# A z unit moved ahead of the last head's gates in a one-core encoder layer

## The chip, the core and the metric

The kernel runs on one core of a Trainium2 chip. The metric is the device time of one execution in microseconds (us). Five engines matter here: PE (TensorE, matrix products and transposes), DVE (VectorE), ACT (ScalarE), POOL (GpSimd, used here almost only to issue DMAs) and SP (SyncE, which issues most of the weight loads). Each engine works through its own instructions in the order in which the program puts them.

## The reference

One encoder layer on a sequence of 512 tokens of width 1024, all in float32:

```
mod = silu(c) @ ada_w + ada_b            # six vectors: shift1, scale1, gate1, shift2, scale2, gate2
h = rmsnorm(x, norm_mix_w) * (1 + scale1) + shift1
z, xbc, dt_raw, q, f_fwd, f_bwd, i, g = split(h @ w_in)
y_ssd = ssd_mixer(z, xbc, dt_raw, ...)   # 16 heads x 64, both directions, gated by silu(z), normed
y_hg = hgrn2_mixer(q, f_fwd, f_bwd, i, g, ...)   # 8 heads x 128, both directions, normed, gated by silu(g)
x = x + gate1 * (concat(y_ssd, y_hg) @ w_out)
h = rmsnorm(x, norm_mlp_w) * (1 + scale2) + shift2
x = x + gate2 * (relu(h @ w_up) ** 2 @ w_down)
return rmsnorm(x, final_norm_w)
```

For one HGRN2 head, forget gates `f` give decays, the keys are built from `f`, `i` gives the values V, and the state is a sum of decayed outer products of keys and values.

## The kernel before

**Units.** The input projection is cut into units of 256 weight columns, listed in `seq` and worked through by `do_unit`. A unit is named by kind and number: `i` gives the values V of two heads, `h0`, `h1`, `h2` give the gates and queries of a pair of heads, `g` and `z` the two output gates, `x` the channels of the SSD group. Heads are numbered 0 to 7; `h0 3` holds both gates of head 6, `h1 3` the queries of heads 6 and 7, `h2 3` both gates of head 7. A unit is 96 matmuls with 256 columns (`i`, `z`, `g`) or 48 with 512 (`h`, `x`). Every weight is split into two parts, `hi` (ACT) and `lo` (DVE), and each product is three matmuls. The weights of the next unit are loaded by SP into four buffers `raw` while a unit runs.

**Streams.** All other work of the mixers is written as generators: `hg_head` for a head, `ssd_group` for the SSD scan, `mix_early` and `mix_late` for the norms and transposes ahead of the output projection, `ada_sums` with `ada_gate` and `ada_T` for the vectors `gate1`, `shift2` (in the code `b2`), `scale2` (`a2`) and `gate2`. Between matmuls of a unit `tick` lets such a generator go one step on, by a hand-kept model of the engines' time (`Clock`). PE's instructions stay in exactly this order. The order on DVE, ACT and POOL is set by the tile scheduler from the same program.

**A head's end.** After seven levels on `Q2`, `K2` and `T`, a head transposes `K2` into `kt` (PE `ps_tr<-cm,K2`, ACT copies), multiplies `kt` with V (`ps_tr<-V,kt`), copies the products to S (ACT), chains them (four DVE instructions `S<-S,T`), and forms its output in `ps_sc` from `V,at` and `S,Q2`. Where a later unit needs the buffers, `ensure(hd, n)` runs a head's remaining steps at once:

```
                if what == "ff":
                    ensure(hd - 2, 99)
                    ensure(hd - 1, 2)
```

This is lines 1083 to 1085, in the h units: the gates of head 7 force the end of head 5, those of head 6 the end of head 4.

**The sums.** `ada_sums` makes 512 columns of one of the vectors on DVE: eight instructions `ada<-adaw,cact`, two for each of four loads `adaw` of 512 KB, which POOL issues into two buffers. The third load waits until the first two instructions are done, the fourth until the fourth is done. A transpose by four matmuls (`ps_tr<-ones,ada`) or one product (`ps_tr<-ada,ones`) ends a sum, and the next sum writes the same tile `ada`. The sums for gate1 (two), b2 (two) and a2 (two) may begin once head 6 is done, since they use its buffers. None begins in the last four of the sixteen steps of the output projection (line 1220). What is left of them is done at once by `bga.drain()` (line 1471), behind the first of four 256-column strips (`ps_sc`, `ps_y`, `ps_mm`, `ps_mm`; 48 matmuls each, weights `wohi`, `wolo`) that end the output projection. The vector a2 and b2 are used right after, in `h2_tile`.

Of the kernel before, what the change touches and what calls it, by code (L numbers as in the profile page):

```python
# [151 lines left out]
def encoder_layer(  # L152
# [8 lines left out]
    clock = Clock()  # L161
# [47 lines left out]
    def const(shape, name, dt=F32):  # L209
        return consts.tile(shape, dt, tag=name, name=name)  # L210
# [400 lines left out]
    def unit_load(src, cols, k0=0):  # L611

        ncols = sum(n for _, n in cols)
        quarters = []
        for q in range(4):
            raw = wp.tile([P, 544], F32, tag="raw", name=nm("raw"), bufs=4)
            v = raw[:, :2 * ncols].rearrange("p (k n) -> p k n", n=ncols)
            o = 0
            for c0_, n in cols:
                r = (k0 + 2 * q) * P  # L620
                nc.sync.dma_start(out=v[:, :, o:o + n], in_=src[r:r + 2 * P, c0_:c0_ + n].rearrange("(k p) n -> p k n", p=P))
                o += n
            quarters.append(v)
        return quarters, ncols

    def unit_split(u, qs=range(4)):
        quarters, ncols = u
        return [split(quarters[q], 2, ncols) for q in qs]
# [231 lines left out]
    def hg_head(hd, hs_):  # L860
# [78 lines left out]
                PE.transpose(out=pt[:, j * P:(j + 1) * P], in_=K2[:, half, cc * P:(cc + 1) * P], identity=ident)  # L939
            A.copy(out=kt[:, 3 * half:3 * half + 3, :], in_=pt[:, :384].rearrange("p (c n) -> p c n", n=P))  # L940
        yield
        while hd // 2 not in vready:
            yield 0.5
        vh = vpair[hd // 2][:, :, (hd % 2) * P:(hd % 2 + 1) * P]
        pts = []
# [40 lines left out]
    def hg_norm(h0, n):  # L986

        r = const([P, NT, 8], "hg_r")
        rr = r[:, :, h0:h0 + n]
        A.activation(rr, hg_ssq[:, :, h0:h0 + n], AF.Sqrt, scale=1.0 / P, bias=epsc)  # L990
        V.reciprocal(out=rr, in_=rr)
        for cc in range(NT):
            yv = hg_y[:, cc, h0 * P:(h0 + n) * P].rearrange("p (h v) -> p h v", v=P)
            V.tensor_tensor(out=yv, in0=yv, in1=rr[:, cc, :].unsqueeze(2).broadcast_to([P, n, P]), op=MULT)
# [3 lines left out]
    def mix_T(grp, j):  # L998
        src = xs if grp == 0 else hg_y
        wcol = vcol("ssdn", j) if grp == 0 else vcol("hgn", 0)  # L1000
        pt = psum("tr")
        for tt in range(NT):
            PE.transpose(out=pt[:, tt * P:(tt + 1) * P], in_=src[:, tt, j * P:(j + 1) * P], identity=ident)
        hi, lo = m_hi[grp][:, j, :], m_lo[grp][:, j, :]
        A.activation(hi, pt, AF.Copy, scale=wcol)
        V.scalar_tensor_tensor(out=lo, in0=pt, scalar=wcol, in1=hi.bitcast(F32), op0=MULT, op1=SUB)

    def mix_early():

        hg_norm(0, 6)  # L1010
        yield
        for j in range(6):
            mix_T(1, j)
            yield
# [4 lines left out]
    vpair, vready, heads = {}, set(), {}  # L1019
# [10 lines left out]
    def do_unit(kind, arg, w, last):  # L1030
# [46 lines left out]
        else:  # L1077
            for j, (what, hd) in enumerate(hparts(kind, arg)):
                hs_ = heads.setdefault(hd, {})
                if j:  # L1080
                    pend.append(last)
                o = mm_T(w, j, h_hi, h_lo, hook=tick)
# [3 lines that stand above are left out]
                hg_evac(hd, what, o, hs_)  # L1086
                hs_["n"] = hs_.get("n", 0) + 1
                if hs_["n"] == 3:
                    ensure(hd - 2, 99)
                    steps[hd] = 0  # L1090
                    hs_["gen"] = counted(hd, hg_head(hd, hs_))
                    sth[hd % 2].add(hs_["gen"], hs_["q"], hs_["K2"], hs_["T"])
                tick()

    steps = {}
# [10 lines left out]
    def ensure(hd, n):  # L1106

        if hd < 0:
            return
        st_ = sth[hd % 2]  # L1110
        while steps.get(hd, 1000) < n and st_.advance():
            pass
# [7 lines left out]
    def hparts(kind, pr):  # L1120
# [4 lines left out]
    seq = [("i", 0), ("h0", 0), ("h1", 0), ("x", 1), ("g", 0), ("h2", 0), ("x", 2),  # L1125
# [4 lines left out]

    def ucols(u):
        k, a = u
        if k in ("h0", "h1", "h2"):
            return [(cols[w_] + hd * P, P) for w_, hd in hparts(k, a)]
        cl = [(cols[k] + a * 256, 256)]
        if u == ("i", 0):
            cl.append((O_DT, 16))
        return cl

    w = unit_split(unit_load(w_in2, ucols(seq[0])))  # L1140
    for i, u in enumerate(seq):
        nw = []
        if i + 1 < len(seq):
            nxt = unit_load(w_in2, ucols(seq[i + 1]))
            nw = unit_split(nxt, range(3))
        if u == ("i", 1):
            ensure(1, 99)
        if u == ("i", 2):
            ensure(3, 99)
        if u == ("i", 3):  # L1150
            ensure(5, 99)
        if u[0] == "z" and not z_phase[0] and (u[1] == 2 or not sts.gens):
            z_phase[0] = True
            sts.drain()
            ssds.close()
            ypl = yps.enter_context(tc.tile_pool(name="ypl", bufs=1, side="right", reuse_waits="tile"))
            m_hi[1] = ypl.tile([P, KD, T], F32R, tag="B_hi", name="m_hi1")
            m_lo[1] = ypl.tile([P, KD, T], F32R, tag="B_lo", name="m_lo1")
            ensure(5, 99)
            stc.add(mix_early())  # L1160

        def last():
            if nw:
                nw.extend(unit_split(nxt, range(3, 4)))
        do_unit(u[0], u[1], w, last)
        w = nw
# [446 lines left out]
    for fb_ in range(NF):  # L1613
        for s_ in range(NS):
            g = fb_ * NS + s_
# [79 lines left out]
```

## Time and profile before

| | |
|---|---|
| median of 3 runs | 976.21 us (974.95 to 1007.0) |
| the profiled execution's own time | 975.98 us |
| its span, first to last instruction | 974.2 us (1.8 us lie outside the span) |
| mean granted TensorE clock | 0.991 |
| PE busy | 937.1 us (96%) |
| weight loads of PE (PEld) | 816.6 us (84%) |
| DVE busy | 729.4 us (75%) |
| ACT busy | 535.5 us (55%) |
| POOL busy | 48.0 us (5%) |

PE is busy nearly all the time, so the places where it is not are few and can be read one by one. In the rows of the trace in order of time, the columns are the start and the duration in us, engine, line of the kernel, operation, output<-input, and the count of instructions merged into the row; in brackets stand the idle time of the engine just before and what released it. All instructions of PE have line 170 or 175 and those of DVE and ACT line 106, since helpers issue them, so the tiles' names tell the place. In a name the buffer's number is left out (K and Q are `K2` and `Q2`).

### The profile page before, as it was taken

The numbers are of one execution on the slowest core, as the hardware profiler recorded it, in microseconds if no ns is written. First come the engines' busy times: TensorE is split into PE (matmuls) and PEld (weight loads), VectorE is DVE, ScalarE is ACT, GpSimd is POOL, SyncE is SP. The second block draws the span as 40 slices with busy tenths as digits, with TensorE's granted clock in tenths as the row PEclk, the third lists the DMA queues.
The fourth block names the chain that finished last, engine by engine and source line by source line (L and its number), as shares of the span: only waits on it lengthen the run. The fifth ranks groups of instructions, "written<-read, shape, count | busy, mean of one in ns | idle before, by whom it ended". The sixth has DMA issues, their size and how long they took to land.

```text
span 974.2 us, 17637 instructions
## 1 busy us (share of the span) xinstructions
PE 937.1 (96%) x6846; PEld 816.6 (84%) x6846; DVE 729.4 (75%) x1269; ACT 535.5 (55%) x1007; POOL 48.0 (5%) x91
## 2 busy tenths in 40 slices
PE   5999999999999999989999999889999999999997
PEld 4788887788877887879997899878799889889987
DVE  4588869787989586867866676897788568667845
ACT  6367647756676466565655324746237326523824
POOL 0000000011000000000111210000000000000000
PEclk8999999999999999999999999999999999999999
DMA  8963422334422343222556786425324313512222
GB/s 270 261 156 84 115 77 59 94 88 125 123 68 67 106 127 94 66 76 67 182 166 187 265 277 190 140 89 161 97 87 141 108 34 108 162 56 87 87 66 87
DMA packets 111865, 119.33 MB, mean 122 GB/s; under 512 B 8188, under 2 KB 93349, under 8 KB 111781
## 3 DMA queue, kind: packets, MB, share of 16 engines
q1 hardware_dynamic: 103285, 89.07, 31.5%
q0 software_dynamic: 8064, 28.32, 9.4%
q8 instruction: 54, 0.88, 0.4%
q10 hardware_dynamic: 432, 0.82, 0.2%
q14 instruction: 30, 0.25, 0.1%
HBM read 116.01 MB, written 2.16 MB: 121 GB/s over the span
## 4 chain that ended last, share of the span: by engine, by line
PE 83%; DVE 6%; ACT 4%; DMA 4%; issue 2%; SPq 1%; DVEq 0%; ACTq 0%; POOLq 0%
PE ps_mm L170 44%; PE ps_sc L170 24%; PE ps_y L170 9%; PE ps_tr L170 4%; PE ps_tr L175 1%; DMA e<-cdr 1%; DVE t L106 1%; DVE lo L106 1%; ACT hi L106 1%; DMA raw<-in_w_out_dram 1%; DMA xe<-in_w_up_dram 1%; DVE x L106 1%; ACT xn L106 1%; DVE ada L106 1%; SPq L230 1%
## 5 line engine op out<-in xcount | busy, mean ns | idle before, releaser
L106 ACT CAST hi<-raw 128x512 fp32r<-128x512 f32 (+1 forms) x220 | 132.3, 612 | 159.4 <-PE ps_sc L170 74.9
L106 DVE TENSOR_TENSOR lo<-raw,hi 128x512 fp32r<-128x512 f32 (+1 forms) x220 | 146.2, 679 | 85.0 <-ACT hi L106 83.5
L170 PE MATMUL ps_mm<-hi,h_hi 128*128 128x256 f32 (+1 forms) x384 | 114.3, 298 | 0.0
L106 ACT CAST hi<-xr 128x512 fp32r<-128x512 f32 x100 | 59.1, 619 | 90.1 <-PE ps_y L170 41.3
L170 PE MATMUL ps_mm<-lo,h_hi 128*128 128x256 f32 (+1 forms) x384 | 108.2, 282 | 0.0
L170 PE MATMUL ps_mm<-hi,h_lo 128*128 128x256 f32 (+1 forms) x384 | 108.1, 282 | 0.0
L170 PE MATMUL ps_mm<-h_hi,hi 128*128 128x512 f32 x256 | 107.4, 420 | 0.0
L170 PE MATMUL ps_mm<-h_lo,hi 128*128 128x512 f32 x256 | 101.2, 395 | 0.2 <-DVE h_lo L106 0.2
L170 PE MATMUL ps_mm<-h_hi,lo 128*128 128x512 f32 x256 | 101.2, 395 | 0.0
L106 DVE TENSOR_TENSOR lo<-xr,hi 128x512 fp32r<-128x512 f32 x100 | 66.5, 686 | 21.6 <-ACT hi L106 21.0
L170 PEld LDWEIGHTS ps_mm<-hi,h_hi 128*128 128x128 f32 x384 | 72.4, 189 | 3.5 <-issue 1.7
L170 PEld LDWEIGHTS ps_mm<-lo,h_hi 128*128 128x128 f32 x384 | 72.5, 189 | 1.9 <-issue 1.7
L170 PEld LDWEIGHTS ps_mm<-hi,h_lo 128*128 128x128 f32 x384 | 72.4, 189 | 0.0
L170 PEld LDWEIGHTS ps_mm<-h_hi,hi 128*128 128x128 f32 x256 | 48.2, 188 | 15.6 <-issue 2.3
L170 PEld LDWEIGHTS ps_mm<-h_lo,hi 128*128 128x128 f32 x256 | 48.2, 188 | 11.7 <-issue 1.4
L170 PEld LDWEIGHTS ps_mm<-h_hi,lo 128*128 128x128 f32 x256 | 48.1, 188 | 10.9
L106 DVE SCALAR_TENSOR_TENSOR ada<-adaw,cact,ada 128x512 f32<-128x512 f32 x56 | 42.0, 749 | 16.1 <-DMA adaw<-in_ada_w_dram 15.4
L170 PE MATMUL ps_mm<-hi,uh 128*128 128x512 f32 (+1 forms) x144 | 50.3, 349 | 0.9 <-DVE t L106 0.9
L106 DVE TENSOR_TENSOR Q<-Q,T 128x512 f32<-128x512 f32 x56 | 42.0, 750 | 11.6 <-PE ps_sc L170 11.5
L170 PE MATMUL ps_mm<-hi,ul 128*128 128x512 f32 (+1 forms) x144 | 49.4, 343 | 0.0
L170 PE MATMUL ps_mm<-lo,uh 128*128 128x512 f32 (+1 forms) x144 | 49.2, 342 | 0.0
L106 ACT ACT_TABLE_LOAD x37 | 47.5, 1283 | 1.4 <-PEq L1682 0.7
(362 smaller groups left out, 2507.5 us busy)
## 6 DMA issues: line engine op xcount, KB each, us to landing
raw<-in_w_in_dram SPq DMA_DIRECT2D x68, 256.0 KB, 3.1
adaw<-in_ada_w_dram POOLq DMA_DIRECT2D x32, 512.0 KB, 5.1
raw<-in_w_down_dram SPq DMA_DIRECT2D x64, 256.0 KB, 2.9
xr<-in_w_up_dram SPq DMA_DIRECT2D x30, 512.0 KB, 3.8
raw<-in_w_in_dram SPq DMA_DIRECT2D x104, 128.0 KB, 2.7
ada_in<-in_ada_w_dram SPq DMA_DIRECT2D x16, 512.0 KB, 6.0
e<-cdr POOLq DMA_DIRECT2D x32, 256.0 KB, 3.7
raw<-in_w_out_dram SPq DMA_DIRECT2D x32, 256.0 KB, 5.0
```

The lines of the kernel that those rows point to most:

```text
L106: return f(*args, **kw)
L170: return tc.keep_in_program_order(nc.tensor.matmul(**kw))
L175: return tc.keep_in_program_order(nc.tensor.transpose(**kw))
L230: nc.sync.dma_start(out=raw[:, :n], in_=w_in2[kc * P:(kc + 1) * P, c0_:c0_ + n])
```

## The change

Four edits. The unit `z 0` stands ahead of `h2 3` in `seq`, where it stood behind `i 3`. A head's products with V are put off while the modelled time of V's copy plus 1.0 lies ahead of PE's modelled time. At the start of the z phase `ensure(5, 99)` is gone, and `mix_early` waits in its place until heads 4 and 5 are through.

```diff
@@ hg_head
-        while hd // 2 not in vready:
+        while hd // 2 not in vready or clock.at(vpair[hd // 2]) + 1.0 > clock.pe:
             yield 0.5
         vh = vpair[hd // 2][:, :, (hd % 2) * P:(hd % 2 + 1) * P]
@@ mix_early
+        while min(steps[4], steps[5]) < 1000:
+            yield 0.5
         hg_norm(0, 6)
@@ seq
-           ("h0", 3), ("h1", 3), ("g", 3), ("h2", 3), ("i", 3),
-           ("z", 0), ("z", 1), ("z", 2), ("z", 3)]
+           ("h0", 3), ("h1", 3), ("g", 3), ("z", 0), ("h2", 3), ("i", 3),
+           ("z", 1), ("z", 2), ("z", 3)]
@@ start of the z phase
-            ensure(5, 99)
             stc.add(mix_early())
```

No instruction is added or removed; what changes is the order. A program with the third and fourth of the named edits alone (no `ensure(5, 99)`, the wait in `mix_early`) has the rows of before on PE and DVE, and a program without these two has the rows of the change: in both orders heads 4 and 5 are through before the z phase begins. On SP the four loads of z 0 now stand ahead of the eight of h2 3 and the four of i 3.

The first place is PE at the end of head 5. Before, in `h2 3`, its last steps stand in one piece behind the first gate's product (`ps_mm`):

```order
L170 MATMUL ps_sc_4627<-Q_674_3852,K_647_3697 64x64 x8
L175 MATMUL ps_tr_4644<-cm,K_647_3697 128x128 x3
L175 MATMUL ps_tr_4649<-cm,K_647_3697 128x128 x3
L170 MATMUL ps_tr_4654<-V_3802,kt_4643 128x128 x3
L170 MATMUL ps_tr_4658<-V_3802,kt_4643 128x128 x3
L170 MATMUL ps_sc_4669<-V_3802,at_3919 128x128
L170 MATMUL ps_sc_4669<-S_4662,Q_674_3852 128x128
```

In the change they are spread over the second half of `z 0`, with twelve or more matmuls between two of them. These are the rows from the products with V:

```order
L170 MATMUL ps_tr_4724<-V_3802,kt_4697 128x128 x3
L170 MATMUL ps_tr_4728<-V_3802,kt_4697 128x128 x3
L170 MATMUL ps_sc_4739<-Q_757_4309,hy_4679 64x64 x8
L170 MATMUL ps_mm_4632<-hi_4292,h_hi 128x256
L170 MATMUL ps_mm_4632<-lo_4293,h_hi 128x256
L170 MATMUL ps_mm_4632<-hi_4292,h_lo 128x256
L170 MATMUL ps_mm_4632<-hi_4292,h_hi 128x256
```

Twelve 256-column and six 512-column matmuls stand there ahead of the outputs from `S,Q2`. For head 4 the products with V moved likewise: before they stood right behind the last matmul of `i 2`, whose result is V; now they stand inside `h0 3`, behind eighteen of the 48 matmuls, and six more 512-column matmuls stand between them and the head's outputs, which line 1084 forces there.

The second place is DVE at the end of head 7, in the z units. Before, the four instructions `S<-S,T` stand ahead of the sum for the second half of gate1 (`ada_5512`):

```order
L106 SCALAR_TENSOR_TENSOR S_5488<-S_5488,T_5361 128x128 x4
L106 TENSOR_TENSOR hold_5205<-hold_5205,ps_tr_5495 128x512
L106 TENSOR_SCALAR ada_5512<-adaw_5513,cact 128x512
L106 SCALAR_TENSOR_TENSOR ada_5512<-adaw_5513,cact,ada_5512 128x512
L106 SCALAR_TENSOR_TENSOR ada_5512<-adaw_5515,cact,ada_5512 128x512 x2
```

In the change they stand among the instructions of that sum (`ada_5609`) on its third and fourth loads:

```order
L106 TENSOR_SCALAR ada_5609<-adaw_5610,cact 128x512
L106 SCALAR_TENSOR_TENSOR ada_5609<-adaw_5610,cact,ada_5609 128x512
L106 SCALAR_TENSOR_TENSOR ada_5609<-adaw_5612,cact,ada_5609 128x512 x2
L106 TENSOR_TENSOR xs<-xs,t_5626 128x2x256
L106 SCALAR_TENSOR_TENSOR ada_5609<-adaw_5690,cact,ada_5609 128x512
L106 SCALAR_TENSOR_TENSOR S_5639<-S_5639,T_5554 128x128
L106 SCALAR_TENSOR_TENSOR ada_5609<-adaw_5690,cact,ada_5609 128x512
L106 SCALAR_TENSOR_TENSOR S_5639<-S_5639,T_5554 128x128 x2
L106 SCALAR_TENSOR_TENSOR ada_5609<-adaw_5694,cact,ada_5609 128x512
```

The first S row now stands behind the first instruction on the third load, the last S row behind the first instruction on the fourth.

The third place is the end of the output projection, behind the first strip (`ps_sc_6575` before, `ps_sc_6552` in the change). Before, PE has one set of four matmuls there, the last a2 sum's:

```order
L170 MATMUL ps_sc_6575<-wohi_6485,m_hi_5000 128x256
L170 MATMUL ps_sc_6575<-wolo_6486,m_hi_5000 128x256
L170 MATMUL ps_sc_6575<-wohi_6485,m_lo_5001 128x256
L170 MATMUL ps_tr_6632<-ones,ada_6218 128x1 x4
L170 MATMUL ps_y_6660<-wohi_6251,m_hi_5000 128x256
```

In the change both a2 sums end there, since head 6 ends one unit later and with it the start of all the sums:

```order
L170 MATMUL ps_sc_6552<-wohi_6462,m_hi_5132 128x256
L170 MATMUL ps_sc_6552<-wolo_6463,m_hi_5132 128x256
L170 MATMUL ps_sc_6552<-wohi_6462,m_lo_5133 128x256
L170 MATMUL ps_tr_6609<-ones,ada_6195 128x1 x4
L170 MATMUL ps_tr_6632<-ones,ada_6615 128x1 x4
L170 MATMUL ps_y_6660<-wohi_6228,m_hi_5132 128x256
```

On DVE all eight instructions of the second of them (`ada_6615`) stand behind the reading of the first one's result (`a<-ps_tr`):

```order
L106 TENSOR_TENSOR t_6601<-ps_sc_6552,hold_5607 128x256
L106 TENSOR_TENSOR a_671<-ps_tr_6609,vt 128x4
L106 TENSOR_TENSOR x_6115<-x_6115,t_6601 128x256
L106 TENSOR_SCALAR ada_6615<-adaw_6616,cact 128x512
L106 SCALAR_TENSOR_TENSOR ada_6615<-adaw_6616,cact,ada_6615 128x512
L106 RECIPROCAL rs_6504<-rs_6504 128x1
L106 SCALAR_TENSOR_TENSOR ada_6615<-adaw_6618,cact,ada_6615 128x512
L106 TENSOR_SCALAR xn_6502<-x_6115,rs_6504 128x512
L106 SCALAR_TENSOR_TENSOR ada_6615<-adaw_6618,cact,ada_6615 128x512
L106 SCALAR_TENSOR_TENSOR ada_6615<-adaw_6622,cact,ada_6615 128x512 x2
L106 SCALAR_TENSOR_TENSOR ada_6615<-adaw_6626,cact,ada_6615 128x512 x2
L106 TENSOR_TENSOR a_671<-ps_tr_6632,vt 128x4
```

Before, the corresponding sum (`ada_6218`) is spread over the stretch of the output projection ahead of the strips (its columns 512 to 767), and this place holds the sum for the first half of gate2 (`ada_7597`), whose product stands much later on PE.

## The prediction

> **What bounds the kernel now.** I read the page first, then the list of PE's waits, then the timeline of PE where it waits.
>
> ```profile
> PE 937.1 (96%) x6846; PEld 816.6 (84%) x6846; DVE 729.4 (75%) x1269; ACT 535.5 (55%) x1007; POOL 48.0 (5%) x91
> PE 83%; DVE 6%; ACT 4%; DMA 4%; issue 2%; SPq 1%; DVEq 0%; ACTq 0%; POOLq 0%
> ```
>
> The first row is busy time, the second the chain that ended last. PE carries the time; an edit that moves its work gains only what PE loses in waiting, and costs whatever new waiting it makes. So I price waits, each at its place. In the stretch that the change reorders (heads 4 to 7 and the output projection, 357 to 620 us) PE waits here:
>
> ```profile
> 359.21 1.78 PE L170 MATMUL ps_tr<-V,kt 128*128 128x128 f32 x8 [1.92 <-ACT V L106]
> ...
> 419.81 0.87 PE L175 MATMUL ps_tr<-cm,K 128*128 128x128 f32 x6 [0.80 <-DVE K L106]
> 420.92 1.60 PE L170 MATMUL ps_tr<-V,kt 128*128 128x128 f32 x12 [0.24 <-ACT kt L106]
> ...
> 425.10 0.46 PE L170 MATMUL ps_sc<-S,Q 128*128 128x128 f32 x2 [2.35 <-DVE S L106]
> ...
> 488.63 1.13 PE L170 MATMUL ps_tr<-ada,ones 128*128 128x512 f32 x2 [0.62 <-ACT S L106]
> ```
>
> The first is head 4, whose products follow the last matmul of V; the next three are head 5, ended in one piece; the last is a sum's product queued behind head 7's copies. Together 5.9 us, 0.6% of the time: that is all that the change can win directly.
>
> **Head 5: -3.4 us.** The three waits (0.80 + 0.24 + 2.35) come from work done at once. In the order of the change twelve 256-column matmuls stand between the transposes and the products with V, and a level product, twelve such matmuls and six 512-column ones behind them.
>
> ```profile
> 394.47 0.28 PE L170 MATMUL ps_mm<-lo,h_hi 128*128 128x256 f32 x1
> 394.59 0.27 PE L170 MATMUL ps_mm<-hi,h_lo 128*128 128x256 f32 x1
> ...
> 388.21 0.39 PE L170 MATMUL ps_mm<-h_lo,hi 128*128 128x512 f32 x1
> 388.44 0.39 PE L170 MATMUL ps_mm<-h_hi,lo 128*128 128x512 f32 x1
> ```
>
> Start to start these are 0.12 and 0.23 us, so the cover is 1.4 us for kt and over 2.8 us for S, against waits of 0.24 and 2.35. I take the whole 3.4; the bounds are 1.0 (a queue on DVE in z 0 eats most of the cover of S) and 3.4. The z unit's own work is the same wherever it stands. Its four loads go ahead of eight others on SP's queue and need the same buffers; PE waits for no weight part in this stretch, so I cost them at nothing; without that cover a late load of such a unit would cost about the page's median landing.
>
> **Head 4: -1.6 us.** The wait for V goes, but what is late next? In the new order PE meets the SSD products, eighteen matmuls, the products with V, six matmuls, then S.
>
> ```profile
> 385.12 1.10 PE L170 MATMUL ps_y<-xs,e 128*64 128x64 f32 x32
> 386.15 1.98 PE L170 MATMUL ps_sc<-st,ct 128*128 128x512 f32 x4
> 387.57 0.79 PE L170 MATMUL ps_mm<-h_hi,hi 128*128 128x512 f32 x1
> ...
> 392.25 0.69 PE L170 MATMUL ps_sc<-Q,hy 128*64 128x64 f32 x16
> ...
> 359.71 0.69 DVE L106 TENSOR_TENSOR lo<-raw,hi 128x512 fp32r<-128x512 f32 x1
> ...
> 366.39 0.69 DVE L106 TENSOR_TENSOR e<-e,off 128x512 f32<-128x512 f32 x1
> 367.00 0.68 DVE L106 TENSOR_TENSOR xs<-xs,t 128x512 f32<-128x512 f32 x1
> ...
> 423.56 1.39 DVE L106 SCALAR_TENSOR_TENSOR S<-S,T 128x128 f32<-128x128 f32 x4 [3.00 <-ACT S L106]
> ...
> 369.72 0.38 PE L170 MATMUL ps_sc<-V,at 128*128 128x128 f32 x2
> ```
>
> PE is free at 359.21 - 1.92 = 357.3; SSD products 387.57 - 385.12 = 2.45; eighteen matmuls 4.1; a level product 0.6; products with V 422.36 - 420.92 = 1.4 by the rows of head 5; six matmuls 1.4; the first output product 0.2: it asks for S at about 367.5. On DVE the new order puts thirteen instructions between the last `lo` (done 360.4) and S, at about 0.61 start to start: S begins at 368.3 and ends at 369.7. So 2.2 us of waiting for S take the place of the 1.92 for V. Before, PE began these outputs at 369.72 with six 512-column matmuls of the unit still behind them (1.4 us); now it begins them at 369.7, with none behind. With the 0.2 us of the first V product already done, that is 1.6 us earlier. Bounds: 0, if the wait for S is 1.6 us longer, and 3.7, if S is in time.
>
> **Head 7: +1.9, and the product behind it -0.6 us.** The 0.62 at 488.63 goes, since that product no longer stands behind head 7's. But S now waits in DVE's queue behind the sum.
>
> ```profile
> 490.52 0.48 DVE L106 TENSOR_SCALAR ada<-adaw,cact 128x512 f32<-128x512 f32 x1
> ...
> 498.95 0.75 DVE L106 SCALAR_TENSOR_TENSOR ada<-adaw,cact,ada 128x512 f32<-128x512 f32 x1 [0.71 <-DMA adaw<-in_ada_w_dram]
> DMA to landing us min/median/max: 3.9/5.1/7.4
> ```
>
> From the product's start to the sum's first instruction 490.52 - 488.63 = 1.9 us; the fourth load's first instruction comes 8.4 us after that; the last S behind it ends another 1.0 us later: 11.3. PE has the product (1.1), 24 matmuls (2.9), transposes (0.9), products with V (1.4), 24 matmuls (2.9), 0.2: 9.4. It waits 1.9 us. Bounds 0 (loads at the fast end) and 4.2 (the last at 7.4 instead of 5.1).
>
> **The end of the output projection: +15.3 us.** This is the largest term. PE's queue now holds two sums' matmuls between the first and the second strip. The second sum writes the tile that the first one's matmuls read, so all eight of its instructions come after them, and PE, whose order is fixed, stands until they are done. The trace shows what such a sum takes at this very place, since gate2's stands there before:
>
> ```profile
> 593.38 0.95 PE L170 MATMUL ps_tr<-ones,ada 128*128 128x1 f32 x8
> ...
> 598.78 0.41 DVE L106 TENSOR_TENSOR t<-ps_sc,hold 128x256 f32<-128x256 f32 x1
> 599.11 0.14 DVE L106 TENSOR_TENSOR a<-ps_tr,vt 128x4 f32<-128x4 f32 x1
> ...
> 599.63 0.48 DVE L106 TENSOR_SCALAR ada<-adaw,cact 128x512 f32<-128x512 f32 x1
> ...
> 605.40 0.75 DVE L106 SCALAR_TENSOR_TENSOR ada<-adaw,cact,ada 128x512 f32<-128x512 f32 x1 [2.61 <-DMA adaw<-in_ada_w_dram]
> ...
> 608.16 0.76 DVE L106 SCALAR_TENSOR_TENSOR ada<-adaw,cact,ada 128x512 f32<-128x512 f32 x1 [0.68 <-DMA adaw<-in_ada_w_dram]
> 601.20 0.71 POOL L436 DMA_DIRECT2D adaw<-in_ada_w_dram  x1 [17.66 <-DVE rs L106]
> 603.08 0.72 POOL L436 DMA_DIRECT2D adaw<-in_ada_w_dram  x1 [1.18 <-DVE ada L106]
> ```
>
> DVE reaches the place 5 us after PE (599.1 against 594.3), as it still has evacuations and weight parts to do; the work on DVE ahead of it is the same in the change (one sum there either way), so I keep 599.6. Two loads are there; the third is issued at 601.2, when its buffer comes free, and used at 605.4; the fourth lets its first instruction begin at 608.16, and two instructions at 0.67 and 0.75 end the sum at 609.6. PE stands from 594.3 to 609.6: 15.3 us. The second set of matmuls itself adds nothing, since the first has only moved here. Bounds: 10.2, if DVE has caught up and begins the sum at 594.5, and 17.6, with a landing of 7.4.
>
> [...]
>
> **The clock behind the gap: +1.6 us.** The granted clock halves behind some of the waits:
>
> ```profile
> 360.00:361.00 1.00, 1.00 (x7) 0.78 (x8) 0.77 (x3) 0.27 (x1) 0.00 (x0) 0.50 0.77 194
> ...
> 363.00:364.00 1.00, 1.00 (x3) 0.52 (x4) 1.00 (x3) 0.00 (x0) 0.54 (x1) 1.00 0.43 144
> ...
> 638.97 0.39 PE L170 MATMUL ps_y<-m_hi,lo 128*128 128x256 f32 x1 [2.32 <-DVE lo L106]
> ...
> 640.00:641.00 1.00, 1.00 (x7) 1.00 (x6) 1.00 (x3) 0.00 (x0) 0.00 (x0) 0.50 0.08 16
> ```
>
> In these stretches of 1 us the seventh figure is the clock: 0.50 after the waits of 1.92 and 2.32, full again some 3.2 us later, so about 1.6 us of work lost. A gap of 15 us will surely do it. Bounds 0 and 1.7. [...]
>
> **What the gap gives back: -3.6 us.** Behind the strips PE waits for the norm of the new x:
>
> ```profile
> 601.79 1.12 PE L175 MATMUL ps_tr<-cm,xn 128*128 128x128 f32 x8 [0.66 <-ACT xn L106]
> 610.43 1.09 PE L175 MATMUL ps_tr<-cm,xn 128*128 128x128 f32 x8 [1.85 <-ACT xn L106]
> 616.88 0.39 PE L170 MATMUL ps_mm<-m_hi,hi 128*128 128x256 f32 x1 [0.71 <-ACT m_hi L106]
> 617.61 0.38 PE L170 MATMUL ps_mm<-m_lo,hi 128*128 128x256 f32 x1 [0.34 <-DVE m_lo L106]
> ```
>
> All four (3.56) come from DVE's lag of 5 us, which the gap clears. Bounds: 0, and 8.0 if the wait of 2.32 at 638.97 and two smaller ones near it go too; they come from DVE's own work there, so I leave them in.
>
> **Sum.** -3.4 - 1.6 + 1.9 - 0.6 + 15.3 + 1.6 - 3.6 = +9.6 us on the profiled execution's 975.98, which lies 0.23 us from the median: 985.6 us, 1.0% slower.
>
> **Rivals.**
>
> - *The gap is not on the path.* If PE finds the second sum ready, as it finds a2's last sum at 593.38 before, the last three terms fall away, and 975.98 - 3.7 = 972.3 us remain, faster by 0.4%. For it speaks that the second sum's first two loads can be there early; against it that the tile is single, so the sum cannot start before PE's first set. 0.10.
> - *The heads' waits come back elsewhere.* If S of head 5 is as late as S of head 4 and each new wait of 2 us halves the clock for 3.2 us (1.6 each, heads 4 and 7), the gain of 3.4 shrinks to 1.0 and 3.2 are added: 985.6 + 2.4 + 3.2 = 991.2. For it speaks the clock behind 359.21; against it that the wait of 2.35 at 425.10 is followed by a full clock. 0.16.
> - *Slower by over 2%.* The sum's loads: if DVE reaches the place later by as much as PE is early, and both awaited loads land at 7.4, the gap is 17.6, and with nothing given back the total is 985.6 + 2.3 + 3.6 = 991.5; only with the second rival on top, 997, does it pass 995.5. 0.04.
> - *The change does less than it says:* two of the four edits move nothing, as the order shows. This costs nothing and is part of every case.
>
> **Chances and range.** The forecast, 0.70: with a gap of 10.2 it gives 980.5, with one of 17.6 it gives 987.9, and the heads' bounds add some 2 us on either side, so 978 to 990; the first three rivals 0.10, 0.16 and 0.04. The range takes 977 to 993, that is the forecast and most of the second rival; the first, at 972, stays out. Since 2% is about what a measurement of this kernel can tell from no change: faster 0.01, same 0.95, slower 0.04.
>
> **What would show it.** Right: a wait of about 15 us on PE for DVE `ada` between the first and second strip, a clock of 0.50 for some 3 us behind it, no wait over 0.5 us for xn behind that; no three waits in a row for K, kt and S of head 5; waits of about 2 us for S at heads 4 and 7. Wrong: matmuls of the strips running on without a gap, which would make the time about 972; a gap of 10 us, if DVE had no lag, which would make it about 980.

## The result and the profile after

| | before | the change |
|---|---|---|
| median | 975.58 us (6 runs) | 993.17 us (6 runs, 992.15 to 994.8) |
| ratio | | 1.0172, 95% interval 1.0154 to 1.0191 |
| the profiled execution's own time, span | 975.98, 974.2 us | 992.15, 990.4 us |
| mean granted TensorE clock | 0.991 | 0.981 |

The change makes the kernel 1.7% slower. The forecast was 1.0% slower, 985.6 us, and the measured median lies just above the upper end of its range, 993. The slowdown is below the 2% within which the forecast put 0.95 of its chances; the interval is 0.4% wide, so a measurement of this kernel tells far smaller differences apart than the 2% that the forecast named for it. (The two medians give 1.0180, inside the interval.) Runs over 1.5% above the fastest of the same kernel, here one of before with 1007.0 us, are left out of the ratios here and below.

The page's rows of busy time and of the chain that ended last, of the change:

```profile
PE 940.4 (95%) x6846; PEld 820.4 (83%) x6846; DVE 730.8 (74%) x1269; ACT 534.6 (54%) x1007; POOL 48.0 (5%) x91
PE 78%; DVE 8%; DMA 6%; ACT 4%; issue 3%; SPq 0%; DVEq 0%; ACTq 0%; POOLq 0%
```

PE has the same 6846 matmuls and is busy for 3.3 us more, though no matmul was added: the granted clock was lower, 0.981 against 0.991. In the chain PE's share fell from 83 to 78%, and DVE and DMA took it over. The waits of PE, from its timeline in the change:

```profile
369.48 0.46 PE L170 MATMUL ps_sc<-S,Q 128*128 128x128 f32 x2 [1.39 <-DVE S L106]
503.46 0.46 PE L170 MATMUL ps_sc<-S,Q 128*128 128x128 f32 x2 [2.34 <-DVE S L106]
511.49 0.50 PE L170 MATMUL ps_mm<-hi,m_hi 128*128 128x512 f32 x1 [2.24 <-ACT t L106]
532.96 1.31 PE L175 MATMUL ps_tr<-cm,xs 128*128 128x128 f32 x8 [1.05 <-DVE m_lo L106]
541.95 1.05 PE L170 MATMUL ps_tr<-ones,ada 128*128 128x1 f32 x8 [0.57 <-DVE m_lo L106]
594.51 0.95 PE L170 MATMUL ps_tr<-ones,ada 128*128 128x1 f32 x8
610.63 1.86 PE L170 MATMUL ps_tr<-ones,ada 128*128 128x1 f32 x8 [15.17 <-DVE ada L106]
```

The three waits of head 5, the wait for V of head 4, the one for a product behind head 7's copies and all four behind the strips are gone. New are the two waits for S (heads 4 and 7), the gap of 15.17 us between the last two sets of `ones,ada`, all three foreseen, and the waits for ACT's `t` at 511.49 and for `m_lo` at 532.96, which the forecast did not have. (`t` is what ACT writes when it empties a bank of products, `xn` the normed new x, `m_hi` and `m_lo` are the two parts of a stage's input, `lo` is the second part of a weight, and `r` a product of the first MLP stage ahead of its relu.)

To see where the time went, the program is cut at three matmuls that stand at the same place of the work in every kernel. The first row below is the first matmul of the output projection before; then come, for the change, that matmul and the first one of the stage behind the strips (before, it is the row at 616.88 in the prediction). The third cut is the set of `ones,ada` behind the first strip, at 594.51 above and at 593.38 in the prediction.

```profile
512.58 0.40 PE L170 MATMUL ps_mm<-hi,m_hi 128*128 128x512 f32 x1
```
```profile
508.39 0.40 PE L170 MATMUL ps_mm<-hi,m_hi 128*128 128x512 f32 x1
634.06 0.28 PE L170 MATMUL ps_mm<-m_hi,hi 128*128 128x256 f32 x1
```

| stretch (us) | before | the change | difference | forecast |
|---|---|---|---|---|
| start to output projection | 512.58 | 508.39 | -4.2 | -3.7 |
| from there to the set of `ones,ada` behind the first strip | 80.80 | 86.12 | +5.3 | 0 |
| from there to the stage behind the strips | 23.50 | 39.55 | +16.05 | 15.3 + 1.6 - 3.6 = +13.3 |
| from there to the last instruction | 357.3 | 356.3 | -1.0 | 0 |
| sum | | | +16.2 | +9.6 |

The sum is that of the two profiled executions; the medians differ by 17.6. The forecast failed in the second row, and by less in the third.

### The profile page after: what moved, and what is told of

Same layout as the page of the kernel before. It is cut to its first block, busy times and chain, and to the rows that moved or that the text cites. A ratio compares the mean times of both kernels' runs of the same rounds, so it can differ in the third digit from the quotient of the medians.

```text
span 990.4 us, 17626 instructions
## 1 busy us (share of the span) xinstructions
PE 940.4 (95%) x6846; PEld 820.4 (83%) x6846; DVE 730.8 (74%) x1269; ACT 534.6 (54%) x1007; POOL 48.0 (5%) x91
## 4 chain that ended last, share of the span: by engine, by line
PE 78%; DVE 8%; DMA 6%; ACT 4%; issue 3%; SPq 0%; DVEq 0%; ACTq 0%; POOLq 0%
PE ps_mm L170 41%; PE ps_sc L170 23%; PE ps_y L170 9%; PE ps_tr L170 4%; DMA adaw<-in_ada_w_dram 3%; DMA raw<-in_w_in_dram 1%; DVE ada L106 1%; DVE lo L106 1%; PE ps_tr L175 1%; ACT hi L106 1%; DVE t L106 1%; DMA e<-cdr 1%; DMA raw<-in_w_out_dram 1%; DMA raw<-in_w_up_dram 1%; ACT xn L106 1%
```

## The experiments

Each kernel's ratio is to before, measured on the same chip. Kernels with the same instructions up to the output projection reached it anywhere from 508.4 to 514.4 us in their traces, and a trace is one execution, so effects of a few us are read from the stretches of the table above, and the ratios only where the effect is larger than some 3 us.

### Each half alone

Only the edit on V's copy (the line in `hg_head`), and only the edit on `seq`:

```diff
-        while hd // 2 not in vready:
+        while hd // 2 not in vready or clock.at(vpair[hd // 2]) + 1.0 > clock.pe:
```

> Before, with only the edit that holds a head's products with V until the modelled time of V's copy. Theory: no gap behind the first strip (one set of ones,ada there); at head 4 a wait for S of 1.4 us, as in the trace of the change, stands in place of the 1.92 for V and the half clock of 3.4 us behind it; head 5 keeps its three waits. 975.6 - 1.92 + 1.39 - 1.5 (the half clock) - 0.6 (products no longer waiting) = 973.0 us, plus or minus 1.2. Rival (the prediction's first working, without the clock): 974.0. Rival (the later end of head 4 pushes a later wait by as much): 975.6.

Measured: ratio 0.9972, interval 0.9958 to 0.9987. PE's waits at heads 4 and 5:

```profile
370.04 0.46 PE L170 MATMUL ps_sc<-S,Q 128*128 128x128 f32 x2 [1.70 <-DVE S L106]
416.38 1.60 PE L170 MATMUL ps_tr<-V,kt 128*128 128x128 f32 x12 [0.24 <-ACT kt L106]
420.55 0.46 PE L170 MATMUL ps_sc<-S,Q 128*128 128x128 f32 x2 [2.35 <-DVE S L106]
```

The wait for V is replaced by one of 1.70 for S, without a stretch of half clock behind it (the mean granted clock is 0.995 against 0.991); there is no gap. Of head 5's three waits the one for K is gone too, and an earlier one for xn behind the strips (0.66 before), while a wait of 0.62 for ACT's S appears at 462.15. 0.9972 of 975.6 is 972.9, the theory's 973.0, but the interval (971.5 to 974.3) also holds the first rival, 974.0 without the clock. This edit alone is a small gain, and the fastest kernel of this study.

```diff
-           ("h0", 3), ("h1", 3), ("g", 3), ("h2", 3), ("i", 3),
-           ("z", 0), ("z", 1), ("z", 2), ("z", 3)]
+           ("h0", 3), ("h1", 3), ("g", 3), ("z", 0), ("h2", 3), ("i", 3),
+           ("z", 1), ("z", 2), ("z", 3)]
```

> Before, with only the unit z 0 moved in front of the eighth head's gates. Theory (the move alone delays the end of head 6 and with it all sums): two sets of ones,ada behind the first strip with a wait for ada of about 15 us, three waits of head 5 gone, wait for V of head 4 kept or turned into one at the copy's end: 994 us, plus or minus 2. Rival (the gap takes both edits): no wait for ada, 975.6 - 3.4 = 972.2 us.

Measured: 1.0117, interval 1.0082 to 1.0153, that is 987 where before is 975.6; 994 was expected. The waits of PE:

```profile
359.45 0.82 PE L170 MATMUL ps_tr<-V,kt 128*128 128x128 f32 x5 [2.16 <-ACT V L106]
510.74 0.50 PE L170 MATMUL ps_mm<-hi,m_hi 128*128 128x512 f32 x1 [1.38 <-ACT t L106]
608.38 1.87 PE L170 MATMUL ps_tr<-ones,ada 128*128 128x1 f32 x8 [15.78 <-DVE ada L106]
```

The move of z 0 alone makes the gap. Against the whole change it lacks head 7's wait for S (2.34), 0.86 of the wait for `t`, and the stretch of half clock behind that wait (512.75 to 516.16 in the change): its output projection up to the gap takes 83.14 us against 86.12. On DVE, this kernel has head 7's four S together, ahead of the sum's instruction on its third load at 501.50:

```profile
498.53 1.22 DVE L106 SCALAR_TENSOR_TENSOR S<-S,T 128x128 f32<-128x128 f32 x4
```

The order on PE differs as well: here the sum's product stands behind head 7's transposes (494.00 and 492.40), in the change ahead of them (492.22 and 494.50). So the edit on V, a gain by itself, seems to cost something once z 0 is moved: head 7's products stand behind the sum's, its S falls in among the sums' instructions, and what follows head 7 comes late (its norm on ACT at 509.23, here at 506.92). The ratios bear this out only just: the interval of the change, 1.0154 to 1.0191, begins where this one ends.

### The gap behind the first strip

The limit for starting a new sum set later, so that one set only stands behind the strip:

```diff
-            ada_on[0] = i < 12 or not ada_idle[0]
+            ada_on[0] = i < 14 or not ada_idle[0]
```

> The change, with the limit for starting a new sum in the output projection set two steps later (14 instead of 12 of sixteen), so that the first a2 sum ends inside the output projection, as before the change, and one sum is left behind the first strip. Theory (the gap is a queue of two sums in one tile): PE's wait of 15.2 us for ada goes, and with it the half clock from 598.1 to 618.6 in the trace of the change, which cost PE about 3.3 us of work; the waits for xn and m_hi behind the strips come back (3.6 us in the trace of before). 993.2 - 15.2 - 3.3 + 3.6 = 978.3 us, plus or minus 1.5. Rival (DVE is late there whatever stands in its queue, and the gap only collects it): a wait for ada of 5 to 10 us stays, and the time is 983 to 988.

Measured: 1.0079, interval 1.0051 to 1.0107, or 983.3 where before is 975.6. The theory, 978.3, missed. The rival's range holds the time, and a wait of 5 us stays, but not where the rival had it. PE's rows at the last two sets:

```profile
573.86 1.84 PE L170 MATMUL ps_tr<-ones,ada 128*128 128x1 f32 x8 [5.41 <-DVE ada L106]
605.20 0.95 PE L170 MATMUL ps_tr<-ones,ada 128*128 128x1 f32 x8
```

The last sum is ready when PE asks for it. The wait is at the sum before it, which is now ended at once after the sixteenth step, 5.41 us too early for it; the clock is halved for 6.8 us there. Of the waits behind the strips 2.0 us come back (0.95 for xn, 0.70 for m_hi, 0.34 for m_lo). Sums that start late are waited for wherever the program ends them.

All sums allowed only after head 7, which puts three sets behind the strip:

```diff
-        if hd == 6:
+        if hd == 7:
```

> The change, with all the sums allowed only after head 7 instead of head 6: three sets of ones,ada then stand behind the first strip on PE, and no sum stands among head 7's S on DVE. Theory (each sum queued there costs PE its whole length): the gap grows by one sum, 10.0 us of DVE by the trace of the change and 1.9 for a set on PE, to about 27; in return the wait for S of 2.3 at head 7, the 2.24 for t at the start of the output projection and the half clock behind that (1.6) go: 993.2 + 11.9 - 6.1 = 999, ratio 1.023, plus or minus 0.003. Rival (the gap is one fixed lag of DVE that any number of sums fits into): the gap stays near 15, ratio 1.011.

Measured: 1.0205, interval 1.0188 to 1.0221, or 995.6 where before is 975.6. PE's rows at head 7's outputs, at the start of the output projection and at the second and third set behind the strip:

```profile
498.68 0.39 PE L170 MATMUL ps_sc<-S,Q 128*128 128x128 f32 x2
508.46 0.50 PE L170 MATMUL ps_mm<-hi,m_hi 128*128 128x512 f32 x1 [1.22 <-ACT t L106]
604.01 1.87 PE L170 MATMUL ps_tr<-ones,ada 128*128 128x1 f32 x8 [14.73 <-DVE ada L106]
616.47 1.84 PE L170 MATMUL ps_tr<-ones,ada 128*128 128x1 f32 x8 [10.59 <-DVE ada L106]
```

One more sum in the queue is one more wait of 10.6 us, the length of a sum, so the first 14.7 fits a sum of 10 and a lag of 5, as the forecast had it. The first row has no wait in brackets: with no sum among them on DVE, head 7's S are in time. Of the wait for `t` half stays.

The last set of `ones,ada` on PE put behind the second strip, the sum itself issued where it was (`ada_n` counts the multiplications of the sums that are issued, 48 in all):

```diff
         if tt == 0:
-            bga.drain()
+            while ada_n[0] < 48:
+                bga.advance()
+        if tt == 1:
+            bga.drain()
```

> The change, with the last set of ones,ada on PE put behind the second strip instead of the first; the sum on DVE is issued at the same place as in the change. Theory (the gap is the time from PE's arrival to the sum's end, and anything put into it is free): one strip of 48 matmuls at 0.118 us, 5.7 us, runs inside the gap; the wait for ada falls from 15.2 to about 9.5, the half clock behind it stays; 993.2 - 5.7 = 987.5, ratio 1.0113. Rival (the second strip's evacuation and norm stand behind the sum on DVE, so that PE waits for xn later by what it gained): ratio 1.015 to 1.017.

Measured: 1.0105, interval 1.0079 to 1.0132, the theory's 1.0113. PE's row:

```profile
617.10 1.86 PE L170 MATMUL ps_tr<-ones,ada 128*128 128x1 f32 x8 [10.11 <-DVE ada L106]
```

The strip runs inside the gap; 10.11 are left of 15.17, and no wait for xn comes back. So the gap lies on the path, and what is put into it is free.

### What sets the sum's start

The last sum in a tile of its own:

```diff
-    ada_tile[1] = lambda: mp.tile([P, T], F32, tag="ada", name=nm("ada"))
+    n_acc = [0]
+    def acc_tile():
+        n_acc[0] += 1
+        return xn2[:, 3, T:] if n_acc[0] == 2 else mp.tile([P, T], F32, tag="ada", name=nm("ada"))
+    ada_tile[1] = acc_tile
```

> The change, with the last a2 sum in a tile of its own (the free half of the last row of xn), so that it need not wait for PE's first set of ones,ada. Theory (DVE's queue, 5 us behind PE, sets when the sum starts; the single tile does not): the sum starts some 1.3 us earlier than in the trace of the change, only because it now stands ahead of the strip's evacuation on DVE; the wait of 15.2 becomes 13.5 to 14.5, ratio 1.016. Rival (the single tile holds the sum): the sum starts with its first loads in place, before 595 us, the wait falls to 9 or 10, ratio 1.011 to 1.012.

Measured: 1.0181, interval 1.0165 to 1.0196. PE's row, DVE's where the sum begins (its tile is called xn here), and ACT's just before:

```profile
612.16 1.83 PE L170 MATMUL ps_tr<-ones,xn 128*128 128x1 f32 x8 [16.07 <-DVE xn L106]
```
```profile
602.04 0.15 DVE L106 TENSOR_SCALAR ssq<-ssq 128x1 f32<-128x1 f32 x1 [0.40 <-ACT xn L106]
602.11 0.48 DVE L106 TENSOR_SCALAR xn<-adaw,cact 128x512 f32<-128x512 f32 x1
```
```profile
601.07 0.84 ACT L106 ACTIVATE xn<-x 128x768 f32<-128x768 f32 x1 [0.21 <-DVE x L106]
```

With this tile the sum still starts 7.0 us after PE's first set (595.14); in the change it starts 6.1 us after it (600.59 against 594.51). That the gap would shorten to 13.5 to 14.5 was wrong. But the kernel does not settle what holds the sum. Its tile is columns 512 to 1023 of the last row of xn, and the squares that ACT forms for the norm write columns 0 to 767 of that row (`row_head`). The ACT row above is the fourth such write, hence of that row; it ends at 601.91, and the sum begins at 602.11. So the sum was cut loose from one tile and tied to another. What the trace of the change itself shows is that its tile is free when PE's first set ends, at 595.46, and that DVE takes up the sum 5.1 us later, with 0.9 us of idle time in between: for so long it is DVE's queue that holds it. Whether a tile that nobody else uses would let it start earlier stays open.

### The clock behind the gap

PE kept busy in the gap by 58 matmuls that the result does not need:

```diff
             acc = yield from ada_sums(which, q)
+            if which == 4 and q == 1:
+                pw = psum("tr")
+                for _ in range(58):
+                    PE.matmul(out=pw, lhsT=m_hi[1][:, 1, :P], rhs=m_hi[1][:, 0, :], start=True, stop=True)
```

> The change, with 58 matmuls of 512 columns between the two last sets of ones,ada on PE, into a bank that nobody reads; this adds work that the result does not need, so that PE is busy for about 13.4 us of the 15.2 us gap. Theory (the clock halves because PE is idle, and stays halved for 8 us behind the gap): the sum on DVE ends at the same time, the granted clock stays at 1.00 through the strips, and 3.3 us come back: 993.2 - 3.3 = 989.9 us, plus or minus 0.7. Rival (the half clock behind the gap costs nothing, since PE would then wait for the norm of the new x, as it did for 3.2 us before the change): waits of 2 to 3 us for xn or m_hi appear behind the strips, and the time stays within 0.7 us of 993.2.

Measured: 1.0168, interval 1.014 to 1.0196, the same as the change. In the two-microsecond windows below (the seventh figure is the clock, in brackets the count of matmuls), first the strips of the change, then those of this kernel:

```profile
612.00:614.00 2.00, 2.00 (x11) 2.00 (x10) 1.36 (x5) 0.00 (x0) 0.00 (x0) 0.50 0.76 223
616.00:618.00 2.00, 2.00 (x11) 2.00 (x11) 0.56 (x1) 0.00 (x0) 0.71 (x1) 0.50 0.91 252
620.00:622.00 2.00, 2.00 (x19) 2.00 (x19) 1.15 (x4) 0.00 (x0) 0.72 (x1) 1.00 0.21 72
```
```profile
616.00:618.00 2.00, 2.00 (x19) 2.00 (x18) 1.35 (x4) 0.00 (x0) 0.29 (x1) 1.00 0.81 250
671.60 0.55 PE L170 MATMUL ps_sc<-m_hi,hi 128*128 128x256 f32 x1 [2.02 <-DVE r L106]
```

At half clock PE starts 11 strip matmuls in 2 us, at full clock 19, a loss of 42%; from its return at 610.63 to 618.56 that is 3.3 us. The filled gap has no half clock (1.00 from 616 to 618 us; the 2.71 us for which PE still waits there fall into two slices of 3.41 us, cut as in the last section, and the first, from 610.11, is idle for 55%), and from the second set to the next stage it takes 19.8 us against 23.4. But the total is not less: between the two sets it takes 0.8 more, and behind the strips 2.4 more, of which 1.5 is in waits for DVE: 0.95 more for r (2.02 against 1.07), 0.3 more for lo and 0.31 for m_lo. The theory was right on the clock and wrong on the time; the rival was right on the time, though its waits for xn and m_hi did not come. What keeps the rest of the gain from showing stays open; a stretch of half clock of 3.4 us stands behind the strips in both kernels (from 656.11 in the change, from 671.55 here).

### The start of the output projection

What ACT does when PE waits for `t`, in the change (ACT's timeline):

```profile
506.76 1.15 ACT L106 CAST hi<-raw 128x512 fp32r<-128x512 f32 x2
507.93 1.28 ACT L106 ACT_TABLE_LOAD   x1
509.23 0.30 ACT L106 ACTIVATE hg_r<-hg_ssq,epsc 128x8 f32<-128x8 f32 x1
509.55 1.28 ACT L106 ACT_TABLE_LOAD   x1
510.84 0.60 ACT L106 ACTIVATE t<-ps_mm 128x512 f32<-128x512 f32 x1
```

The last z products leave their bank with the silu at 510.84. Ahead of it stand the norm of heads 6 and 7 and a table load on each side of it. In before the norm stands at 497.32, in a lull; since head 7 ends late, it now falls on the end of the z phase. This kernel ties the norm to the last z unit:

```diff
-        A.activation(rr, hg_ssq[:, :, h0:h0 + n], AF.Sqrt, scale=1.0 / P, bias=epsc)
+        eb = epsc
+        if h0:
+            eb = const([P, 1], "eps_late")
+            V.tensor_scalar(out=eb, in0=zssq[:, 3, 3:4], scalar1=0.0, scalar2=EPS, op0=MULT, op1=ADD)
+        A.activation(rr, hg_ssq[:, :, h0:h0 + n], AF.Sqrt, scale=1.0 / P, bias=eb)
```

> The change, with the norm of heads 6 and 7 tied to the last z unit (its eps is made by one small DVE instruction from a sum that the last z evacuation writes), so that ACT evacuates the last z products first and computes the norm afterwards. The change itself stood at 1.0172 of before. Theory (PE's wait of 2.24 us for ACT's t at the start of the output projection comes from ACT's two table loads and the norm ahead of the evacuation, and half the clock for 3.4 us with it): both go, 2.24 + 1.6 = 3.8 us, ratio 1.013, plus or minus 0.0015. Rival (the start of the output projection is early anyway, and the time comes back at the next wait for m_lo or in the gap behind the first strip, whose end DVE sets): ratio 1.016 to 1.018.

Measured: 1.0168, interval 1.0142 to 1.0194. By the ratio nothing is gained: the theory's 1.013 lies outside the interval, and the rival's range, 1.016 to 1.018, holds the time. The trace shows the wait gone all the same: ACT evacuates first,

```profile
514.43 0.60 ACT L106 ACTIVATE t<-ps_mm 128x512 f32<-128x512 f32 x1
516.72 1.28 ACT L106 ACT_TABLE_LOAD   x1
518.01 0.30 ACT L106 ACTIVATE hg_r<-hg_ssq,eps_late 128x8 f32<-128x8 f32 x1
```

PE has no wait for `t`, and from the first matmul of the output projection to the set behind the first strip it takes 82.54 us (514.23 to 596.77) against 86.12. That is 3.6 of the 3.8 expected. In this trace 0.6 of it went into a longer gap (15.81), and PE reached the output projection 5.8 us later than in the change, with two stretches of half clock on the way, behind the waits for S of heads 4 and 7, that the trace of the change does not have (its mean granted clock is 0.979 against 0.981). So the cost of the norm's place is shown in its own stretch, and not in the time of this kernel, whose five runs spread from 988.7 to 996.4 us.

Then both, the norm tied to the last z unit and the last set behind the second strip, and a third kernel in which the set stands further back, behind 39 of the third strip's 48 matmuls (the expectation says 36; the trace counts 39); the change itself ran beside them. The third kernel's edit, besides the norm's and, behind the first strip, the `while` loop shown above in place of the drain:

```diff
-            if i == 2 and tt >= 2:
-                h2_tile(tt - 2)
+            if i == 12 and tt == 2:
+                bga.drain()
+            if i == 14 and tt == 2:
+                h2_tile(0)
+            if i == 2 and tt == 3:
+                h2_tile(1)
```

> The change itself once more, beside the next two on one chip. Ratio 1.017, plus or minus 0.002; in the trace a gap of 15 to 16 us behind the first strip, a wait of about 2.2 us for ACT's t at the start of the output projection; stretches of half clock that last whole multiples of 3.41 us and start only behind a stretch of 3.41 us in which PE was idle for more than about half.

> The change, with the last set of ones,ada behind the second strip and the norm of heads 6 and 7 behind the last z evacuation. Theory (the two costs lie at different places and add): the first alone stood at 1.0105; the wait for t (2.2) and the half clock behind it (1.5) go as well: ratio 1.0067, plus or minus 0.002. Rival (DVE, not PE, sets the time from the start of the output projection to the sum's end, so an earlier PE only waits longer in the gap): the wait for ada grows from 10.1 to 13 or more, ratio 1.010.

> As the last one, with the last set of ones,ada put further back, behind 36 of the 48 matmuls of the third strip, and the first transposes of the new x behind it. Theory: 84 matmuls of 0.118 us, 9.9 us, lie inside the gap; the wait for ada is 5 to 6 us; 993.2 - 9.9 - 3.7 = 979.6, ratio 1.003. Rival (the transposes of the new x, now later, are what the first product of the next stage waits for): a wait of 2 to 4 us for m_hi or m_lo there, ratio 1.006 to 1.007.

Measured: the change 1.0164 (1.014 to 1.0187), as expected, the two edits together 1.0080 (1.0059 to 1.0101), the third 1.0058 (1.0037 to 1.0078). PE's waits in the three traces:

```profile
511.88 0.50 PE L170 MATMUL ps_mm<-hi,m_hi 128*128 128x512 f32 x1 [2.25 <-ACT t L106]
611.32 1.87 PE L170 MATMUL ps_tr<-ones,ada 128*128 128x1 f32 x8 [15.61 <-DVE ada L106]
```
```profile
606.34 1.87 PE L170 MATMUL ps_tr<-ones,ada 128*128 128x1 f32 x8 [9.55 <-DVE ada L106]
```
```profile
608.97 1.23 PE L170 MATMUL ps_tr<-ones,ada 128*128 128x1 f32 x5 [5.59 <-DVE ada L106]
```

The wait in the gap does not grow when PE needs less time for the output projection (9.55, where 13 or more was the rival's), so in the traces the two costs lie apart. The stretch of the output projection is 82.2 and 82.3 us in the last two. The ratios do not show the norm's part by itself: 1.0080 stands against 1.0105 without the norm's edit, with intervals that overlap. For the third, the theory's 1.003 is missed; 1.0058 is near the rival's 1.006, though not for the rival's reason. In its trace no wait for m_hi or m_lo appears, but from the next stage to the end it takes 2.9 us longer than that of the change; 1.0 of this is the wait for r (2.04), the rest stays open. None of these beats before; the edit on V alone does.

## Why the prediction was right and where it was off

The forecast had the way, the place and the size of the largest cost right, and a slowdown below 2%. Its total was too small: +9.6 us, where the medians differ by 17.6 and the two traces by 16.2.

- *Head 5, -3.4:* right, the three rows are gone. *The product behind head 7's copies, -0.6:* gone.
- *Head 4, -1.6:* right in kind, and the wait for S is 1.39 instead of 2.2. A second gain was left out: before, half a clock for 3.4 us followed the wait for V. *Head 7, +1.9:* 2.34, for the reason given; a sum's instructions stand ahead of S:

```profile
499.61 0.75 DVE L106 SCALAR_TENSOR_TENSOR ada<-adaw,cact,ada 128x512 f32<-128x512 f32 x1 [1.53 <-DMA adaw<-in_ada_w_dram]
502.30 0.75 DVE L106 SCALAR_TENSOR_TENSOR ada<-adaw,cact,ada 128x512 f32<-128x512 f32 x1 [0.49 <-DMA adaw<-in_ada_w_dram]
502.97 0.34 DVE L106 SCALAR_TENSOR_TENSOR S<-S,T 128x128 f32<-128x128 f32 x1
```

  Together -4.2 against -3.7. That these agree so well is in part luck: the five other traces with the same instructions up to the output projection reach it at 508.8 to 514.4 us, from 3.8 earlier to 1.8 later than before. In four of the five, half clock follows head 7's wait (from 503.28 in the kernel with the later limit, from 508.25 in the one with the last set behind the second strip), and in the second of these two head 4's too (from 371.72).
- *The gap, +15.3:* 15.17, made as the forecast said. The sum begins at 600.59 against 599.6, and ends at 610.6 against 609.6, and PE arrives 1.1 us later too. The lag of DVE is there as forecast; how much of the start is due to the single tile no kernel here shows.
- *The step that failed* is what follows head 7. The forecast priced PE's wait for S and stopped there, with nothing for the output projection. But head 7's end releases a norm on ACT, and it and a table load of 1.28 us on each side of it now stand ahead of the evacuation that frees a bank for the output projection: 2.24 us of waiting, about 1.4 of half clock behind it (3.4 us at 42%), and 1.1 more in waits for m_lo, in all most of the 5.3. Tying the norm elsewhere took 3.6 out of this stretch in the trace, though that kernel's time did not fall (1.0168); why not stays open.
- *The clock behind the gap, +1.6,* was mis-sized: 3.3 us, since the half clock lasts 7.9 us after PE's return and not 3.2. *What the gap gives back, -3.6:* all four waits went (3.56), as forecast, and 0.3 of the wait at 634.97.
- *The loads:* in the change the two that DVE waits for are issued at 602.15 and 604.12 and used at 606.29 and 609.04, 4.1 and 4.9 us later, so the third rival's 7.4 did not come.
- Of the rivals, the gap off the path is refuted by its 15.17 and by the kernel whose strip went into it. The second, that the heads' waits come back elsewhere, gave 991.2 and came nearest to the time, but by another mechanism: head 5's S was in time, and in the trace of the change no half clock followed the waits of heads 4 and 7. In other traces it did: in the ten traces of the change and of the kernels built on it, behind head 7's wait in six of the nine that have it (from 503.28, 504.34 and 508.25 in three of them), behind head 4's in three (from 370.12 and 371.72 in two). So this rival's half clock came in some executions and not in others, and some runs of the change may hold it.

## What to carry to other kernels

When a change makes one chain end later, follow what its end releases on every engine, up to the next instruction that somebody waits for; here a norm of 0.3 us with two table loads of 1.28 landed ahead of a bank's evacuation. A sum or a transfer whose result PE asks for in a fixed place costs its whole length plus its engine's lag if it is issued only there (here 10.0 and 5.1 us, a gap of 15.17); put the asking further back, or start it earlier and check that the sum before it is ready too. And two edits that each look local may have a price together that neither has alone: the edit on V gains 0.3% by itself, and on top of the moved unit the time rises from 1.0117 to 1.0164 and 1.0172. The intervals of the first and the last do not meet, by a hair, and those of the first and the second overlap.

## What the hardware showed

In the traces of before and of the change every stretch of half clock away from the end of the span lasts 3.41 us or a whole multiple of it (twice that at the start of each span, 6.83 us from 14.81 and from 14.40; six times behind the gap, 598.08 to 618.56), and within a trace their starts lie whole multiples of 3.413 us apart (in before 359.55 and 639.45, 82.0 of them apart; in the change 512.75, 598.08 and 656.11, 25.0 and 17.0). Cut into slices of this length, PE's busy time (the first figure behind the length) can be read beside the clock (the seventh). Before:

```profile
356.14:359.55 3.41, 1.49 (x13) 1.30 (x13) 3.13 (x7) 2.60 (x6) 0.00 (x0) 1.00 0.21 49
359.55:362.97 3.42, 3.42 (x41) 3.08 (x39) 2.23 (x9) 2.10 (x6) 0.54 (x1) 0.50 0.91 246
420.99:424.40 3.41, 1.76 (x14) 1.57 (x14) 0.80 (x3) 2.89 (x5) 0.00 (x0) 1.00 0.00 0
424.40:427.82 3.42, 2.72 (x21) 2.66 (x22) 0.69 (x3) 0.44 (x4) 0.00 (x0) 1.00 0.02 5
```

The change:

```profile
499.09:502.51 3.42, 2.04 (x18) 1.84 (x16) 2.41 (x6) 0.68 (x2) 0.70 (x1) 1.00 0.53 149
509.33:512.75 3.42, 1.26 (x5) 1.05 (x6) 2.91 (x8) 3.39 (x7) 0.00 (x0) 1.00 0.47 149
512.75:516.16 3.41, 3.41 (x9) 2.67 (x8) 1.58 (x5) 1.97 (x6) 0.00 (x0) 0.50 0.52 154
608.32:611.74 3.42, 1.11 (x6) 1.11 (x6) 1.50 (x2) 0.00 (x0) 1.22 (x2) 0.50 0.53 155
611.74:615.15 3.41, 3.41 (x17) 3.41 (x18) 1.79 (x6) 0.00 (x0) 0.56 (x1) 0.50 0.50 154
615.15:618.56 3.41, 3.41 (x18) 3.41 (x18) 1.37 (x2) 0.00 (x0) 0.86 (x2) 0.50 0.72 169
```

The slices with 1.49 and 1.26 us busy (idle for 56% and 63%) are followed by one at half clock; those with 1.76 and 2.04 (48% and 40%) are not. So the clock was halved behind a wait of 1.92 us and not behind one of 2.35, which falls across two slices. Seven traces were cut in this way between 100 and 700 us: before, the change and its repetition, and the kernels with three sets behind the strip, with the last set behind the second strip, with both edits, and with the set in the third strip. In them 19 slices at full clock were followed by half clock, idle for 54.3% to 100%, and of those that were not, none was idle for more than 53.1%; but in the filled gap the one idle for 55% was not followed by half clock either. Behind the last mostly idle slice of the gaps that ended in a wait of 15.17, 15.61, 10.11, 10.59 and 9.55 us, two further slices pass before the clock is full again, behind the wait of 5.59 us and the shorter ones only one. The slice that holds 607.5 us of the span begins at 605.31 in before, at 604.91 in the change and at 604.78 in its repetition, at 605.64, 607.24, 606.95 and 606.74 in the other four. So where the slices fall differs from trace to trace, and head 7's wait is followed by half clock in some traces (from 508.25, 504.34) and not in others (2.34 us, in the change); an estimate of what a wait of 2 us costs where the clock halves behind it is 1.4 us (42% of 3.41, the loss of the strips).
